# The gate and up projections of a two-FFN encoder layer, taken together in blocks of 512+512 columns, with three of eight pairs of row blocks multiplied by seven block products in place of eight

## The chip, the core and the metric

The kernel runs on one core of one Trainium2 chip. The metric is the time of one execution on the device in microseconds (us). The engines in play are TensorE (PE, matrix products into PSUM), VectorE (DVE), ScalarE (ACT), GpSimd (POOL, here above all the issuer of small transfers) and SyncE (SP, the issuer of the weight loads). The kernel before takes 1782.21 us (median of three runs, 1781.82 to 1783.28).

## What is computed

One encoder layer on 256 tokens of width 2048: a half-weighted SwiGLU feed-forward block, a mixer of two attention groups, a second half-weighted SwiGLU block, and a final norm. The change lies in the two feed-forward blocks, which the reference writes as

```python
def _swiglu(h, w_gu, w_down):
    g, u = jnp.split(h @ w_gu, 2, axis=-1)
    return (jax.nn.silu(g) * u) @ w_down
...
x = x + 0.5 * _swiglu(_rms_norm(x, ffn1_norm[l]), ffn1_w_gu[l], ffn1_w_down[l])
...
x = x + 0.5 * _swiglu(_rms_norm(x, ffn2_norm[l]), ffn2_w_gu[l], ffn2_w_down[l])
```

`w_gu` is 2048 x 11264: its left 5632 columns are the gate, its right 5632 the up projection. `w_down` is 5632 x 2048. All data are float32.

## The kernel before

**Precision.** Every float32 operand is split into a high part rounded to fp32r (`whi`, `xT_hi`, `hT_hi`; ACT casts) and a low part (`wlo`, `xT_lo`, `hT_lo`; DVE subtracts), both by `split` (L128 to L130). A product of two operands is three matmuls into one PSUM bank: high by high (L195), high by low (L196), low by high (L197). One matmul takes a 128x128 block of activations as the stationary operand and streams 512 weight columns.

**A block product.** `mm_block` (L158) runs over the rows of a weight matrix in pairs of 128-row blocks. Each pair of row blocks is one load by SP into a `raw` tile of 128x2x1024 (three such tiles), is split into two `whi` and two `wlo` tiles (four of each, so two pairs of row blocks can be split at a time), and is multiplied with both halves of the tokens (t = 0, 1) and both 512-column halves (b = 0, 1): 2 x 2 x 2 x 3 = 24 matmuls. After the last pair the four PSUM banks are read out by an `evac` function. PSUM has six banks for this (`ps_mm`) and two for everything else (`ps_x`).

**A feed-forward block.** `ffn` (L237) cuts the 5632 columns into groups of 1024 (the last has 512). For each group `gate` runs `mm_block` over the eight pairs of row blocks and ACT writes silu of the bank, scaled by the row norm, to `sg` (L246); `up` does the same with the up columns and DVE multiplies (L261) to `h`. Then `h` is turned: DVE transposes 32x32 squares to `near` (L274), POOL issues 16 small transfers to `turned` (L280), and `split` writes `hT_hi` and `hT_lo`. These steps stand in a list (`pending`) of which `pump` takes one per pair of row blocks. `down` multiplies `hT` with `w_down`, one group behind, in two halves of 1024 output columns, and DVE adds the banks to `x` (L232). The activations `xT_hi`, `xT_lo` have a pool of their own. In the first feed-forward block they are filled from transfers of `xT` through three `raw_x` tiles (`load_xT`, L324) while the first weights arrive.

**What sets the order.** The program is written in the order above, and a scheduler that follows its own timeline of the engines decides in which order each engine's queue gets the instructions (SP is kept in program order in the first gate, PE in the last half of the last `down`). On the chip every engine takes its queue in that fixed order and waits where an operand or a buffer is not ready.

## Time and profile before

| what | value |
|---|---|
| median of three runs | 1782.21 us |
| the profiled execution's own time | 1782.46 us |
| its span, first to last instruction | 1780.7 us |
| PE busy | 1767.7 us (99%) |
| DVE busy | 990.4 us (56%) |
| ACT busy | 829.2 us (47%) |
| granted TensorE clock | 0.999 of 2.4 GHz |
| transfers | 355.72 MB, 200 GB/s on average |

The span is what the trace shows; the 1.8 us by which the execution's own time exceeds it lie outside the first and the last instruction. "Busy" of PE includes matmuls that overlap in its pipeline, so the distance between matmuls, not the length of one, says how fast it runs.

### The profile page before, as it was taken

What the parts mean: (1) busy time and instruction counts of PE and PEld (TensorE: products, weight loads), DVE (VectorE), ACT (ScalarE), POOL (GpSimd) and SP (SyncE); (2) the same over time, 40 slices, a digit from 0 to 9 for tenths busy, and PEclk for the clock granted to TensorE, in tenths of its full rate; (3) what the DMA queues carried; (4) which work ended last, traced back from release to release, by engine and by line L of the source; (5) the groups of instructions that cost most, each with busy time, mean ns of one, the idle gap of its engine ahead of it and who ended that gap; (6) DMA issues with size and microseconds to landing.
All of it is one profiled execution on the core that took longest, in us unless ns stands there. A gap on an engine that the chain in (4) does not pass through costs nothing.

```text
span 1780.7 us, 20561 instructions
## 1 busy us (share of the span) xinstructions
PE 1767.7 (99%) x7864; PEld 1462.4 (82%) x7864; DVE 990.4 (56%) x1147; ACT 829.2 (47%) x1195; POOL 149.5 (8%) x267
## 2 busy tenths in 40 slices
PE   9999999999999999999999999999999999999998
PEld 7888888888888888888788888888888888888886
DVE  6454644645645556745566564555545546545556
ACT  6444443443443443746776454343443443344444
POOL 0010100100100101122110000101001001001010
PEclk9999999999999999999999999999999999999999
DMA  9565655655655676655455545666556556556573
GB/s 342 194 220 189 213 192 197 224 192 189 215 192 194 180 238 204 200 192 194 143 183 199 184 167 193 216 205 214 190 190 219 198 195 213 190 192 220 149 253 118
DMA packets 108418, 355.72 MB, mean 200 GB/s; under 512 B 10992, under 2 KB 15520, under 8 KB 108192
## 3 DMA queue, kind: packets, MB, share of 16 engines
q1 hardware_dynamic: 101360, 341.54, 57.7%
q0 software_dynamic: 6240, 11.57, 2.3%
q8 instruction: 61, 1.00, 0.2%
q10 hardware_dynamic: 720, 1.31, 0.2%
q14 instruction: 37, 0.30, 0.0%
HBM read 337.60 MB, written 2.10 MB: 191 GB/s over the span
## 4 chain that ended last, share of the span: by engine, by line
PE 95%; ACT 1%; DMA 1%; SPq 1%; DVE 1%; issue 1%; POOL 0%; POOLq 0%; ACTq 0%; DVEq 0%
PE psm L196 31%; PE psm L197 31%; PE psm L195 31%; DMA raw<-in_w_in 1%; SPq L456 1%; PE psx L142 0%; PE psx L549 0%; PE psx L564 0%; PE psx L584 0%; ACT heads L425 0%; ACT heads L443 0%; PE psx L513 0%; DMA gain_ffn_norm<-in_ffn_norm 0%; ACT q_sb L422 0%; ACT whi L129 0%
## 5 line engine op out<-in xcount | busy, mean ns | idle before, releaser
L130 DVE TENSOR_TENSOR wlo<-raw,whi 128x1024 fp32r<-128x1024 f32 (+1 forms) x676 | 757.6, 1153 | 703.1 <-ACT whi L129 699.4
L129 ACT CAST whi<-raw 128x1024 fp32r<-128x1024 f32 (+1 forms) x676 | 647.2, 996 | 843.8 <-PE psm L197 780.4
L196 PE MATMUL psm<-wlo,xT_hi 128*128 128x512 f32 x1696 | 659.1, 390 | 0.1
L197 PE MATMUL psm<-whi,xT_lo 128*128 128x512 f32 x1696 | 658.0, 390 | 0.0
L195 PE MATMUL psm<-whi,xT_hi 128*128 128x512 f32 x1696 | 587.7, 390 | 3.0 <-ACT whi L129 1.5
L195 PEld LDWEIGHTS psm<-whi,xT_hi 128*128 128x128 f32 x1696 | 318.2, 188 | 70.2 <-ACT xT_hi L330 2.4
L196 PEld LDWEIGHTS psm<-wlo,xT_hi 128*128 128x128 f32 x1696 | 318.4, 188 | 66.3 <-DVE wlo L130 0.5
L197 PEld LDWEIGHTS psm<-whi,xT_lo 128*128 128x128 f32 x1696 | 318.4, 188 | 65.8
L196 PE MATMUL psm<-wlo,hT_hi 128*128 128x512 f32 x836 | 323.9, 389 | 0.0
L197 PE MATMUL psm<-whi,hT_lo 128*128 128x512 f32 x836 | 323.6, 389 | 0.0
L195 PE MATMUL psm<-whi,hT_hi 128*128 128x512 f32 x836 | 295.4, 389 | 0.0
L280 POOL DMA_DIRECT2D turned<-near x192 | 101.3, 535 | 1204.6 <-DVE near L274 1020.0
L196 PEld LDWEIGHTS psm<-wlo,hT_hi 128*128 128x128 f32 x836 | 157.0, 188 | 32.2
L195 PEld LDWEIGHTS psm<-whi,hT_hi 128*128 128x128 f32 x836 | 157.0, 188 | 32.1
L197 PEld LDWEIGHTS psm<-whi,hT_lo 128*128 128x128 f32 x836 | 157.0, 188 | 31.9
L232 DVE SCALAR_TENSOR_TENSOR x<-psm,x 128x512 f32<-128x512 f32 (+1 forms) x113 | 74.5, 682 | 19.0 <-PE psm L197 17.6
L246 ACT ACTIVATE sg<-psm,rstd 128x512 f32<-128x512 f32 x44 | 28.6, 687 | 12.5 <-PE psm L197 12.5
L261 DVE SCALAR_TENSOR_TENSOR h<-psm,rstd,sg 128x512 f32<-128x512 f32 x44 | 31.6, 737 | 0.0
L130 DVE TENSOR_TENSOR hT_lo<-turned,hT_hi 128x512 fp32r<-128x512 f32 x44 | 30.1, 685 | 0.0
L104 POOL TENSOR_TENSOR rs<-ms,minus_half 128x4 f32<-128x4 f32 (+1 forms) x18 | 20.2, 1120 | 116.6 <-DVE ms L103 116.5
L120 ACT ACTIVATE junk<-x 128x512 bf16<-128x512 f32 (+1 forms) x33 | 20.3, 614 | 16.4 <-DVE x L232 14.2
L274 DVE STREAM_TRANSPOSE near<-h 128x1024 f32<-128x1024 f32 (+1 forms) x24 | 27.7, 1152 | 0.3
(102 smaller groups left out, 390.6 us busy)
## 6 DMA issues: line engine op xcount, KB each, us to landing
raw<-in_ffn_w_gu SPq DMA_DIRECT2D x158, 1024.0 KB, 5.0
raw<-in_ffn_w_down SPq DMA_DIRECT2D x88, 1024.0 KB, 5.1
raw<-in_w_in SPq DMA_DIRECT2D x32, 1024.0 KB, 5.2
raw<-in_ffn_w_gu SPq DMA_DIRECT2D x32, 512.0 KB, 3.7
raw<-in_w_out SPq DMA_DIRECT2D x16, 1024.0 KB, 5.0
turned<-near POOLq DMA_DIRECT2D x160, 64.0 KB, 4.5
raw<-in_w_in SPq DMA_DIRECT2D x8, 512.0 KB, 3.8
heads<-near SPq DMA_DIRECT2D x96, 32.0 KB, 1.9
```

The costliest lines, as they stand in the source:

```text
L104: nc.gpsimd.tensor_tensor(dst, ms[:, :width], minus_half[:, :width], op=ALU.pow)
L120: nc.scalar.activation(junk[:, :c1 - c0], x[t][:, c0:c1], AF.Square, scale=D ** -0.5, accum_out=p[:, n:n + 1])
L129: casts.append(nc.scalar.copy(hi, src))
L130: return nc.vector.tensor_tensor(lo, src, f32(hi), op=ALU.subtract)
L195: nc.tensor.matmul(o, xh, wh, start=k == 0, stop=False)
L196: nc.tensor.matmul(o, xh, wl, start=False, stop=False)
L197: nc.tensor.matmul(o, xl, wh, start=False, stop=k == nk - 1)
L232: nc.vector.scalar_tensor_tensor(x[t][:, s], ps[:, c0:c1], scale, x[t][:, s], op0=ALU.mult, op1=ALU.add)
L246: nc.scalar.activation(sg[t][:, b * 512:(b + 1) * 512], ps, AF.Silu, scale=norm.rstd[t][:, 0:1])
L261: nc.vector.scalar_tensor_tensor(h[t][:, s], ps, norm.rstd[t][:, 0:1], sg[t][:, s], op0=ALU.mult, op1=ALU.mult)
L274: nc.vector.transpose(near[:, t].rearrange("p q (k d) -> p q k d", d=B32), h[t][:, :width].rearrange("p (k q d) -> p q k d", q=Q, d=B32))
L280: nc.gpsimd.dma_start(turned[q * B32:(q + 1) * B32, :, i, :], near[i * B32:(i + 1) * B32, :, q, :])
```

## The change

The first 1024 columns of gate and up are computed as before, with the two halves of the rows in the pool `ht`. While its up part runs, the normalised activations are written once more in two new forms: for five of the eight pairs of row blocks `xs` (the first 128 tokens, the last 128, and their difference), for the other three `xp` (seven 128x128 combinations of the 2x2 square of row blocks and token halves). This is done by `spread`, `normalised`, `single_rows` and `paired_rows`.

The other 9 blocks of 512 columns of each feed-forward block go through `columns`: gate and up columns c0 to c0+511 together, eight loads of a `raw` tile, each now two transfers of one 128-row block with 512 gate and 512 up columns. A pair marked False in `PAIRS` is a single: it is split as before and multiplied in 4 x 2 x 3 = 24 matmuls into the banks `c12`, `c11`, `c3`, `c21`. A pair marked True is multiplied by Strassen's algorithm (Winograd's form): DVE forms four combinations of its four weight squares (`Ta`, `Tb`), these and three plain squares are split, and seven products of three matmuls are added to seven banks (21 matmuls); `p1`, `p6`, `p7` are the three further banks (`p7` lies in `ps_x`). When the last pair's products are done, `done` combines the seven banks with seven DVE adds, two DVE multiplies, one ACT copy and two silu to `h`. `h` is then turned by 512 columns, and takes the turned squares back itself.

```diff
+PAIRS = (False, False, True, False, False, True, False, True)
 MIX_SLOTS = 4
...
-    xt_p = ctx.enter_context(tc.tile_pool(name="xt", bufs=1))
...
+    def new_rows():
+
+        return (ht_p.tile([P, WB // P, T], F32R, name="hT_hi"), ht_p.tile([P, WB // P, T], F32R, name="hT_lo"))
+
+    def rows(sets):
+
+        def at(k, t):
+            return tuple(part[:, k % 8, t * P:(t + 1) * P] for part in sets[k // 8])
+        return at
+
...
+
+
+
+        with tc.tile_pool(name="ffn", bufs=1) as fp:
+            inner = ExitStack()
+            ip = inner.enter_context(tc.tile_pool(name="ffn_in", bufs=1))
+            w_pair = w_gu.rearrange("r (s f) -> r s f", s=2)
+            hT, turned_blocks = {}, set()
+            n_groups = (DFF + WB - 1) // WB
+
+
+            def turn_block(i, h):
+
+                near = fp.tile([P, NT, Q, P], F32, name="near")
+                turned = h.rearrange("p t (i f) -> p t i f", i=Q)
+
...
+                    to = 4 * (i % 2) + k
+                    hi, lo = (part[:, to:to + 2, :].rearrange("p k (i d) -> p i k d", d=B32)
+                              for part in hT[i // 2])
                     with tc.issue_after(splits[-1].ins):
                         split(hi, lo, src)
 
-                pending.extend(functools.partial(turn, t) for t in range(NT))
...
+            if before is None:
+                mm_block(rows(xT), NK, w_gu, 0, 0, WB, evac_gate)
+            else:
+                with tc.manual_schedule(engines={mybir.EngineType.SP}):
+                    mm_block(rows(xT), NK, w_gu, 0, 0, WB, evac_gate, lambda c: before(c, ip), after)
...
+            single = [k for c, pair in enumerate(PAIRS) if not pair for k in (2 * c, 2 * c + 1)]
+            paired = [c for c, pair in enumerate(PAIRS) if pair]
+            xs = [ip.tile([P, len(single), 3, P], F32R, name=f"xs{i}") for i in range(2)]
+            xp = [ip.tile([P, len(paired), 7, P], F32R, name=f"xp{i}") for i in range(2)]
+            rb = fp.tile([P, T], F32, name="rb")
+
+            def spread():
+                near = fp.tile([P, NT, Q, P], F32, name="near")
+                ps = ps_x.tile([P, 512], F32, name="psx")
+                for t in range(NT):
+                    nc.vector.tensor_scalar(near[:, t, 0, :], ident, 0.0, norm.rstd[t][:, 0:1],
+                                            op0=ALU.mult, op1=ALU.add)
+                    nc.tensor.transpose(ps[:, t * P:(t + 1) * P], near[:, t, 0, :], ident)
+                nc.scalar.copy(rb, ps[:, :T])
+
+            def normalised(c):
+                n = ip.tile([P, 2, 512], F32, name="Ta").rearrange("p j (a t) -> p (j a) t", t=T)[:, :2, :]
+                hi, lo = (f32(part[:, 2 * c % 8:2 * c % 8 + 2, :]) for part in xT[2 * c // 8])
+                nc.vector.tensor_tensor(n, hi, lo, op=ALU.add)
+                nc.vector.tensor_tensor(n, n, rb.unsqueeze(1).broadcast_to([P, 2, T]), op=ALU.mult)
+                return n
+
+            def single_rows(c):
+                n = normalised(c)
+                i = single.index(2 * c)
+                diff = ip.tile([P, 2, 512], F32, name="Tb")[:, 0, :2 * P].rearrange("p (k t) -> p k t", t=P)
+                nc.vector.tensor_tensor(diff, n[:, :, :P], n[:, :, P:], op=ALU.subtract)
+                hi, lo = (part[:, i:i + 2, 0:2, :].rearrange("p k a t -> p k (a t)") for part in xs)
+                split(hi, lo, n)
+                split(xs[0][:, i:i + 2, 2, :], xs[1][:, i:i + 2, 2, :], diff)
+
+            def paired_rows(c):
+                n = normalised(c)
+                i = paired.index(c)
+                z = ip.tile([P, 2, 512], F32, name="Tb")[:, 0, :].rearrange("p (a t) -> p a t", t=P)
+                a12, a22, a11, a21 = (n[:, j, t * P:(t + 1) * P] for j in range(2) for t in range(2))
+                nc.vector.tensor_tensor(z[:, 0, :], a21, a22, op=ALU.add)
...
+            pending.append(spread)
+            pending.extend(functools.partial(paired_rows if pair else single_rows, c)
+                           for c, pair in enumerate(PAIRS))
+            ready = []
+            pending.append(lambda: ready.append(True))
+            mm_block(rows(xT), NK, w_gu, 0, DFF, WB, evac_up, slots=2)
+            while not ready:
+                pump()
+            for b in range(2):
+                turn_block(b, h0[b])
+
+
+            def columns(i):
+                c0 = i * 512
+                order = ("c12", "c11", "c3", "c21", "p1", "p6")
+                bank = {n: ps_mm.tile([P, 512], F32, name="psm") for n in order}
+                bank["p7"] = ps_x.tile([P, 512], F32, name="psx")
+                t1 = fp.tile([P, WB], F32, name="sg0")
+                t2 = fp.tile([P, WB], F32, name="sg1")
+                c1, c22, u2, u3 = t1[:, :512], t1[:, 512:], t2[:, :512], t2[:, 512:]
+                h = fp.tile([P, NT, 512], F32, name="h", bufs=2)
+                begun = set()
+
...
+                def done(name):
+                    if name == "p1":
+                        nc.scalar.copy(c1, bank["p1"])
+                    elif name == "p6":
+                        add(u2, bank["p6"], c1)
+                    elif name == "p7":
+                        add(u3, bank["p7"], u2)
+                    elif name == "c12":
+                        add(u2, bank["c12"], u2)
+                        add(c22, bank["c12"], u3)
+                    elif name == "c11":
+                        add(c1, bank["c11"], c1)
+                        nc.scalar.activation(c1, c1, AF.Silu)
+                    elif name == "c3":
+                        add(u2, bank["c3"], u2)
+                        nc.vector.tensor_tensor(h[:, 0, :], u2, c1, op=ALU.mult)
+                    elif name == "c21":
+                        add(u3, bank["c21"], u3)
+                        nc.scalar.activation(u3, u3, AF.Silu)
+                        nc.vector.tensor_tensor(h[:, 1, :], u3, c22, op=ALU.mult)
+
+                for c, pair in enumerate(PAIRS):
+                    raw = raw_p.tile([P, 2, WB], F32, name="raw").rearrange("p j (s f) -> p j s f", s=2)
+                    w = []
+                    for j in range(2):
+                        k = 2 * c + j
+                        loads.append(nc.sync.dma_start(raw[:, j], w_pair[k * P:(k + 1) * P, :, c0:c0 + 512]))
+                    for j in range(2):
+                        hi = whi_p.tile([P, WB], F32R, name="whi").rearrange("p (s f) -> p s f", s=2)
+                        lo = wlo_p.tile([P, WB], F32R, name="wlo").rearrange("p (s f) -> p s f", s=2)
+                        n = 1 if pair and j == 1 else 2
+                        splits.append(split(hi[:, :n], lo[:, :n], raw[:, j, :n]))
+                        w.append([(hi[:, s], lo[:, s]) for s in range(2)])
+                    if not pair:
+                        def xk(j, a):
+                            i_ = single.index(2 * c + j)
+                            return xs[0][:, i_, a, :], xs[1][:, i_, a, :]
+                        for name, a_, s in (("c12", 1, 1), ("c11", 0, 0), ("c3", 2, 1), ("c21", 1, 0)):
+                            mm(name, [(xk(j, a_), w[j][s]) for j in range(2)], False)
+                        pump()
+                        continue
+                    i_ = paired.index(c)
+                    b21, b22, b11, b12 = (raw[:, j, s] for j in range(2) for s in range(2))
+                    tt = []
+                    ta = ip.tile([P, 2, 512], F32, name="Ta")
+                    tb = ip.tile([P, 2, 512], F32, name="Tb")
+
+                    flat = raw.rearrange("p j s f -> p (j s) f")
+                    nc.vector.tensor_tensor(ta, flat[:, 3:4, :].broadcast_to([P, 2, 512]), flat[:, 1:3, :],
+                                            op=ALU.subtract)
+                    nc.vector.tensor_tensor(tb[:, 0], b22, ta[:, 1], op=ALU.subtract)
+                    nc.vector.tensor_tensor(tb[:, 1], b21, tb[:, 0], op=ALU.subtract)
+                    for n, src in (("Ta", ta), ("Tb", tb)):
+                        hi = ip.tile([P, 2, 512], F32R, name=n + "_hi")
+                        lo = ip.tile([P, 2, 512], F32R, name=n + "_lo")
+                        splits.append(split(hi, lo, src))
+                        tt.extend((hi[:, s], lo[:, s]) for s in range(2))
+                    t3, t1_, t2_, t4 = tt
+                    xa = [(xp[0][:, i_, m, :], xp[1][:, i_, m, :]) for m in range(7)]
+                    a12, a22, a11, s1, s2, s3, s4 = xa
+                    product = {"p1": (a11, w[1][0]), "c11": (a12, w[0][0]), "c3": (s4, w[0][1]),
+                               "c21": (a22, t4), "c12": (s1, t1_), "p6": (s2, t2_), "p7": (s3, t3)}
+                    names = (("c11", "c3", "p1", "p7", "c12", "p6", "c21") if c < last else
+                             ("p1", "p6", "p7", "c12", "c11", "c3", "c21"))
+                    for m, name in enumerate(names):
+                        mm(name, [product[name]], c == last)
+                        if c == last:
+                            done(name)
+                        if m == 3:
+                            pump()
+                turn_block(i, h)
...
+                if final:
+                    inner.close()
+                    t_major = last_pools and last_pools(inner)
                 for half in range(2):
-                    evac = last_evac(half) if last and last_evac else add_to_x(half, 0.5)
...
+            for j in range(1, n_groups):
+                for i in range(2 * j, min(2 * j + 2, DFF // 512)):
+                    columns(i)
+                if j < n_groups - 1:
+                    down(j - 1)
+            down(n_groups - 2)
+            down(n_groups - 1)
...
+    xT = [new_rows(), new_rows()]
+
+    def load_xT(c, pool):
+
+        raw = pool.tile([P, 2, 512], F32, name=("Ta", "Tb")[c % 2]).rearrange("p j f -> p (j f)")[:, :2 * T]
+        raw = raw.rearrange("p (j t) -> p j t", j=2)
...
+            hi, lo = (part[:, k % 8, :] for part in xT[k // 8])
+            nc.scalar.activation(hi, raw[:, j, :], AF.Copy, scale=gain1[:, k:k + 1])
+            nc.vector.scalar_tensor_tensor(lo, raw[:, j, :], gain1[:, k:k + 1], f32(hi),
+                                           op0=ALU.mult, op1=ALU.subtract)
```

How the change moves the work is seen at one place on two engines. First the queue of DVE where a stretch of eight row-block pairs ends. Before, at the end of the first `up` (its `h` tiles are h0_497 and h1_498; wlo_788 and wlo_792 are the first split of the next gate):

```order
L130 TENSOR_TENSOR wlo_744<-raw_741,whi_743 128x1024
L130 TENSOR_TENSOR wlo_748<-raw_741,whi_747 128x1024
L130 TENSOR_TENSOR wlo_788<-raw_785,whi_787 128x1024
L130 TENSOR_TENSOR wlo_792<-raw_785,whi_791 128x1024
L261 SCALAR_TENSOR_TENSOR h0_497<-psm_509,rstd0_106,sg0_128 128x512
L261 SCALAR_TENSOR_TENSOR h1_498<-psm_516,rstd1_107,sg1_129 128x512
L261 SCALAR_TENSOR_TENSOR h0_497<-psm_523,rstd0_106,sg0_128 128x512
L274 STREAM_TRANSPOSE near_781<-h0_497 128x1024
L261 SCALAR_TENSOR_TENSOR h1_498<-psm_530,rstd1_107,sg1_129 128x512
L130 TENSOR_TENSOR wlo_827<-raw_824,whi_826 128x1024
```

The four reads of the banks and the first transpose stand together, between plain splits that are one pair of row blocks ahead.

Now the same queue at the change from one block of columns to the next in the first feed-forward block. In the block that ends, psm_1915 to psm_1918 are c12, c11, c3, c21, psm_1920 is p6 and psx_1921 is p7; raw_2262, raw_2299 and raw_2342 are the first three pairs of the next block, the third of them a Strassen pair:

```order
L130 TENSOR_TENSOR Tb_lo_2215<-Tb_2206,Tb_hi_2214 128x1024
L130 TENSOR_TENSOR wlo_2266<-raw_2262,whi_2265 128x1024
L434 TENSOR_TENSOR Ta_2353<-raw_2342 128x1024
L130 TENSOR_TENSOR wlo_2270<-raw_2262,whi_2269 128x1024
L384 TENSOR_TENSOR sg1_1923<-psm_1920,sg0_1922 128x512
L130 TENSOR_TENSOR wlo_2303<-raw_2299,whi_2302 128x1024
L436 TENSOR_TENSOR Tb_2354<-raw_2342,Ta_2353 128x512
L130 TENSOR_TENSOR Ta_lo_2359<-Ta_2353,Ta_hi_2358 128x1024
L384 TENSOR_TENSOR sg1_1923<-psx_1921,sg1_1923 128x512
L384 TENSOR_TENSOR sg0_1922<-psm_1916,sg0_1922 128x512
L130 TENSOR_TENSOR wlo_2307<-raw_2299,whi_2306 128x1024
L437 TENSOR_TENSOR Tb_2354<-raw_2342,Tb_2354 128x512
```

The combining adds (L384) are now woven into the splits of the next three pairs and into the weight combinations of the third. Next the queue of PE at the same two places. Before, the last matmuls of the first gate and the first of its `up` (psm_509, psm_516):

```order
L197 MATMUL psm_169<-whi_464,xT_lo_111 128x512
L196 MATMUL psm_176<-wlo_465,xT_hi_110 128x512
L197 MATMUL psm_176<-whi_464,xT_lo_111 128x512
L195 MATMUL psm_509<-whi_501,xT_hi_110 128x512
L196 MATMUL psm_509<-wlo_502,xT_hi_110 128x512
L197 MATMUL psm_509<-whi_501,xT_lo_111 128x512
L195 MATMUL psm_509<-whi_505,xT_hi_110 128x512
L195 MATMUL psm_516<-whi_501,xT_hi_110 128x512
L196 MATMUL psm_516<-wlo_502,xT_hi_110 128x512
```

The gate's last matmuls and the first of `up` follow each other with nothing between them, and `up` starts on two fresh banks.

Now the last products of the block that ends (psm_1918) and the first of the next (psm_2252 is its c12, psm_2253 its c11, psx_2258 its p7):

```order
L378 MATMUL psm_1918<-Tb_hi_2214,xp0_500 128x512
L380 MATMUL psm_1918<-Tb_lo_2215,xp0_500 128x512
L381 MATMUL psm_1918<-Tb_hi_2214,xp1_501 128x512
L378 MATMUL psm_2252<-whi_2265,xs0_498 128x512
L380 MATMUL psm_2252<-wlo_2266,xs0_498 128x512
L381 MATMUL psm_2252<-whi_2265,xs1_499 128x512
L378 MATMUL psm_2252<-whi_2269,xs0_498 128x512
L378 MATMUL psx_2258<-Ta_hi_2358,xp0_500 128x512
L380 MATMUL psm_2252<-wlo_2270,xs0_498 128x512
L381 MATMUL psm_2252<-whi_2269,xs1_499 128x512
L378 MATMUL psm_2252<-whi_2302,xs0_498 128x512
L378 MATMUL psm_2253<-whi_2265,xs0_498 128x512
```

PE no longer takes a pair of row blocks in one run: it starts the third pair's product (psx_2258) between the matmuls of the first, and begins the banks one after another, as they come free.

## Rows read from the trace of the kernel before

**Rows 1.** Part 1 and part 4 of the page: engines' busy time, chain that ended last

```profile
PE 1767.7 (99%) x7864; PEld 1462.4 (82%) x7864; DVE 990.4 (56%) x1147; ACT 829.2 (47%) x1195; POOL 149.5 (8%) x267
...
PE 95%; ACT 1%; DMA 1%; SPq 1%; DVE 1%; issue 1%; POOL 0%; POOLq 0%; ACTq 0%; DVEq 0%
```

**Rows 2.** The chain in order of time, first gate: start us, us, what

```profile
17.46 0.91 PE psm L195 x4
...
22.90 0.91 PE psm L195 x4
```

**Rows 3.** Instructions by line and shape: count, busy us, mean ns, idle before

```profile
L196 PE MATMUL psm<-wlo,xT_hi 128*128 128x512 f32 x1696 | 659.1, 390 | 0.1
...
L130 DVE TENSOR_TENSOR wlo<-raw,whi 128x1024 fp32r<-128x1024 f32 x588 | 697.6, 1222 | 655.4 <-ACT whi L129 654.6
...
L129 ACT CAST whi<-raw 128x1024 fp32r<-128x1024 f32 x588 | 593.0, 1052 | 783.0 <-PE psm L197 752.4 <-DMA raw<-in_w_in 8.9 <-issue 6.2
...
L130 DVE TENSOR_TENSOR wlo<-raw,whi 128x512 fp32r<-128x512 f32 x88 | 60.0, 691 | 47.7 <-ACT whi L129 44.8 <-PE psm L197 2.7
...
L232 DVE SCALAR_TENSOR_TENSOR x<-psm,x 128x512 f32<-128x512 f32 x111 | 73.7, 687 | 18.8 <-PE psm L197 17.4
...
L261 DVE SCALAR_TENSOR_TENSOR h<-psm,rstd,sg 128x512 f32<-128x512 f32 x44 | 31.6, 737 | 0.0
...
L130 DVE TENSOR_TENSOR hT_lo<-turned,hT_hi 128x512 fp32r<-128x512 f32 x44 | 30.1, 685 | 0.0
...
L274 DVE STREAM_TRANSPOSE near<-h 128x512 f32<-128x512 f32 x4 | 2.8, 702 | 0.0
...
L331 DVE SCALAR_TENSOR_TENSOR xT_lo<-raw_x,gain_ffn_norm,xT_hi 128x256 fp32r<-128x256 f32 x16 | 7.0, 480 | 0.1
...
L441 DVE TENSOR_TENSOR heads<-heads,swapped 128x128 f32<-128x128 f32 x8 | 2.3, 291 | 0.7
...
L142 PE MATMUL psx<-ident,x 128*128 128x128 f32 x64 | 9.2, 272 | 0.0
```

**Rows 4.** DVE in order of time, second gate: start, us, what, idle before

```profile
104.95 2.36 DVE L130 TENSOR_TENSOR wlo<-raw,whi 128x1024 fp32r<-128x1024 f32 x2 [3.08 <-ACT whi L129]
```

**Rows 5.** Stretch, us, busy of PE, PEld, DVE, ACT, POOL (count), clock, DMA share, GB/s

```profile
51.40:95.00 43.60, 43.60 (x194) 36.13 (x193) 21.73 (x21) 18.47 (x20) 0.00 (x0) 1.00 0.58 192
...
182.00:225.50 43.50, 43.50 (x194) 36.03 (x193) 27.33 (x30) 18.10 (x21) 8.43 (x16) 1.00 0.69 218
...
617.00:660.00 43.00, 43.00 (x191) 35.61 (x191) 24.17 (x35) 22.37 (x34) 0.00 (x0) 1.00 0.71 220
```

**Rows 6.** Part 6 of the page: DMA issues, KB each, us to landing

```profile
raw<-in_ffn_w_gu SPq DMA_DIRECT2D x158, 1024.0 KB, 5.0
...
raw<-in_ffn_w_gu SPq DMA_DIRECT2D x32, 512.0 KB, 3.7
...
turned<-near POOLq DMA_DIRECT2D x160, 64.0 KB, 4.5
```

**Rows 7.** Tile `near`: duration of an instruction, ns, min/median/max

```profile
L280 POOL DMA_DIRECT2D turned<-near x192: 533/533/612, 98.7 to 1723.7; - x192
```

**Rows 8.** In order of time, the start of the first gate

```profile
5.78 0.43 SPq L327 DMA_DIRECT2D raw_x<-in_xT  x1
...
6.23 0.89 DVE L331 SCALAR_TENSOR_TENSOR xT_lo<-raw_x,gain_ffn_norm,xT_hi 128x256 fp32r<-128x256 f32 x2
...
13.79 2.00 ACT L129 CAST whi<-raw 128x1024 fp32r<-128x1024 f32 x2 [1.73 <-DMA raw<-in_ffn_w_gu]
```

**Rows 9.** Busy by stretch, the start: columns as in Rows 5

```profile
6.20:12.00 5.80, 5.75 (x25) 4.75 (x26) 5.75 (x11) 5.74 (x12) 0.00 (x0) 1.00 1.05 391
...
12.00:51.00 39.00, 39.00 (x174) 32.31 (x173) 23.34 (x32) 26.31 (x44) 1.29 (x2) 1.00 0.90 335
```

171 lines of the change are left out of this document (75 added, 96 removed).

## The prediction

> **What bounds the kernel now.** Part 1 of the page comes first: TensorE is busy for 1767.7 of 1780.7 us, VectorE for 56%; part 4 agrees, with 95% of the chain of work that ended last on PE [rows 1]. A busy PE need not be a fast one, so the next view is the chain in order of time, in the first gate: one pair of row blocks starts at 17.46 us and the next at 22.90, 5.44 us for 24 matmuls, 0.2267 us each [rows 2]. The mean of 390 ns in the groups by line [rows 3] is longer because neighbours overlap; it prices nothing here. So the time is a number of matmuls times 0.2267 us, as long as the operands are ready.
>
> Whether they stay ready is read from the other engines. In a gate, DVE works 2.36 us on two splits and then waits 3.08 us for ACT's cast [rows 4], which in turn waits for PE to free the split tiles (752 of ACT's 783 us of idle time before this cast) [rows 3]. By stretches, an `up` of 43.6 us has 21.7 us of DVE work and a `down` of 43.5 us has 27.3 [rows 5]. DVE has room of about half its time, and this room is what the change spends.
>
> **What the change removes.** Each of the 9 blocks of columns per feed-forward block, 18 in all, has three Strassen pairs with 21 matmuls where 24 stood: 183 for 192. That is 18 x 9 = 162 matmuls, at 0.2267 us 36.7 us. A block's PE work falls from 43.5 to 41.5 us. On PE come four transposes in `spread`, at 0.272 us [rows 3] 1.1 us.
>
> **What it adds on DVE.** Prices are 1.18 us for a 128x1024 operation (half of 2.36 [rows 4]; 1.222 when it stands alone [rows 3]), 0.69 for 128x512, 0.687 from PSUM, 0.70 for a transpose, 0.685 for an `hT_lo` part [rows 3]. The sum over a block:
> - five singles, two splits each: 5 x 2.36 = 11.8;
> - three Strassen pairs: one and a half splits 1.87, `Ta` 1.18, `Tb` 2 x 0.69, two splits of combinations 2.36, so 6.79 each, 20.4;
> - `done`: seven adds and two multiplies, 9 x 0.69 = 6.2;
> - turning: 2 x 0.70 + 2 x 0.685 = 2.8.
>
> Together 41.2 us, and 42.1 if every operation has its full duration, against 41.5 of PE. In a block of columns DVE is thus as full as PE. Over two blocks and the `down` behind them it is not: that `down` leaves it 16 us (43.5 less 27.3) [rows 5], but with four `whi` and `wlo` tiles it can work only about two pairs of row blocks ahead, so little of this can be saved up. ACT has 24 us per block (ten casts at 1.05, three pairs at 3.8, the rest 3) and is not the bound [rows 3].
>
> **Where the adds wait.** The place to look at is the change of blocks, in the order of the queues. Seven banks are in use and the next block begins while they are read. Its first bank is the one that the ACT copy of p1 frees, its second is that of p6, and I take its third to be that of c11, from the wait that stands at its first matmul. From the end of the split `Tb_lo_2215` to the add on `psm_1916` that frees c11, DVE has five operations of 1.22 and four of 0.69: 8.9 us. PE has 36 matmuls from the one that needs `Tb_lo_2215` to the first in the third bank, 8.2 us. So PE stalls there about 0.7 us, or nothing where DVE was ahead; later in the block DVE is ahead again by the same count. Queued behind that wait on PE is everything else of the block; on DVE, the waits for ACT casts of `Ta` and `Tb` hold up the splits of the next pairs. I take 0.5 us per block, 9 us in all. The ends are 0, and 3.8: DVE's 42.1 us with the three casts of `Ta` at 1.05 us [rows 3] fully exposed makes a block of 45.3 us.
>
> **The first `up` of each feed-forward block** also makes `xs` and `xp`. DVE: 16 splits 18.9; five times `single_rows` at 2 x 0.69 + 0.48 + 0.69 + 0.48 = 3.03 (a 128x256 operation is 0.48), 15.2; three times `paired_rows` at 2 x 0.69 + 4 x 0.29 + 0.58 + 0.69 = 3.81, 11.4 (0.29 for 128x128; 0.58 is set between 0.48 and 0.69) [rows 3]; four reads at 0.737, 2.9. Sum 48.4 against 43.5 of PE, 4.9 too much. The two pairs of lead cover part; I take 3 us for each of the two, between 0 and 10 (10 if the next block's first Strassen preparation of 6.8 falls in front of the end too).
>
> **Loads.** A tile is now filled by two transfers of 512 KB with runs of 512 columns. The last group has such loads already: 3.7 us to landing against 5.0 for 1024 KB [rows 6], and a DMA share of 0.71 at 220 GB/s against 0.58 at 192 in an `up` [rows 5], 7% more engine time per byte. A block needs 8 MB in 41.5 us, 202 GB/s, so a share of about 0.65. I cost it at nothing: three `raw` tiles hide it. If that cover goes, it is a rival below.
>
> **The start.** `load_xT` has two tiles where it had three. The third `raw_x` transfer went out at 5.78 us; now it must wait on SP until the first tile has been read, and DVE does that from 6.23 to 7.12 [rows 8]. The weight loads stand behind it in SP's queue and slip by some 1.4 us. Loads are dense there (share 1.05, then 0.90), yet PE does not idle from 12 to 51 us [rows 9], and the third pair's cast starts at 13.79 [rows 8] for matmuls at 17.46 [rows 2]. I take 1 us, between 0 and 3.
>
> **The sum.** 1780.7 - 36.7 + 9 + 6 + 1.1 + 1 = 1761.1 us of span. The profiled execution's own time was 1.8 us over its span, and the median of the runs lies 0.25 us under it: 1762.6 us.
>
> **A rule against the change.** POOL issues each of the 192 transfers into `turned` in 533 ns, median and minimum alike, at most 612 [rows 7], although DVE operations of 1.2 us run beside them [rows 3]; DVE does not hold them up. By this row the 16 issues of a block take 8.6 us and land 4.5 later [rows 6], 13 us, while some 23 us of DVE work (15 x 1.22 + 7 x 0.69 by its queue) stand between the second transpose and the `hT_lo` part that needs them: hidden. If instead each issue waited out one DVE operation, 16 x (0.533 + 1.22) + 4.5 = 32.5 us, 9.5 too late per block, 171 in all, and 1933 us. The Trainium skill ("SBUF — State Buffer", section "SBUF: two separate sides") says that DVE and GpSimd share one port pair under an exclusive lock, held for a whole instruction, also by DVE operations with two SBUF inputs against a GpSimd operation that reads SBUF. By that rule the 1933 us would come about; the row speaks against it for these issues.
>
> **The rivals.**
> 1. Everything is hidden: DVE's lead of two pairs covers all block changes and the first `up`. 1780.7 - 36.7 + 1.1 = 1745.1 of span, 1746.6 us. For it: DVE's sum of 41.2 is under 41.5, and the order was woven to that end. Against: no reserve at all for a wait.
> 2. Slower: VectorE becomes the bound in the 18 blocks. Place: the Strassen pairs, where `Ta`, its cast and its split follow one another on two engines and block the splits behind them. Price: 45.3 us a block, 3.8 over PE, 68 in all, and 6 us in each first `up`: 1780.7 - 36.7 + 68.4 + 12 + 2.1 = 1826.5, so 1828 us. It decides from 1.6 us of stall per block on, where (36.7 - 8.1) / 18 is used up. For it: full durations alone make 42.1. Against: in the queue the cast and the split are parted by other work.
> 3. The loads: behind a Strassen pair DVE has two singles, 4.7 us, before it needs the tile that this pair frees; the load takes 5.0 [rows 6], 7% more 5.35. Two such places per block, 0.65 each, 23 us beside the stalls above: 1786 us, about no change. Against: DVE is ahead of PE there by some 4 us.
> 4. The port lock above, 1933 us.
>
> **Chances.** The forecast with its neighbours (own range 1750 to 1775 us) 0.56; everything hidden 0.13; VectorE as the bound 0.20, spread from no change up to 1830; the loads 0.09; the lock 0.02. Faster by over 0.2% (the least that a measurement of this kernel tells from no change): 0.56 + 0.13 + 0.01 = 0.70; within 0.2%: 0.07; slower: 0.23. The range of 8 in 10 goes from 1745, where all is hidden, to 1790, which takes in the loads and the milder part of rival 2, the ends of the unknown stalls being 0 and 3.8 us a block.
>
> **What the new profile would show.** PE's count falls from 7864 by 158, and a block of columns lasts 41.5 to 42.5 us, not 43.5 (rival 2: 44 to 46; rival 3: 43). DVE's busy time rises from 990 by some 380 us to about 77%. PE's waits name DVE (`wlo`, `Ta_lo`, or the bank adds) for about 15 us in total; over 35 would make rival 2 right, and waits on loads before `Ta` rival 3. `turned` issues stay at 533 ns. The forecast is wrong if a block of columns is over 43 us, or if PE is held for more than 10 us in a first `up`.

## The result, and the profile after

The changed kernel takes 1763.2 us (median of four runs, 1760.4 to 1770.4), 19 us less than before; the ratio of the runs is 0.9899, with a 95% interval of 0.9869 to 0.9928. The forecast was 1762.6. The profiled execution took 1760.4 us, the fastest of the four, with a span of 1758.6, 22.1 under the span of before.

First the page of after: engines' busy time, the chain that ended last, then groups by line (count | busy us, mean ns of one | idle us before, and what ended most of it), then DMA issues (KB, us to landing).

```profile
PE 1738.5 (99%) x7706; PEld 1430.3 (81%) x7706; DVE 1324.1 (75%) x1633; ACT 931.6 (53%) x1323; POOL 234.7 (13%) x427
...
PE 84%; DMA 6%; DVE 4%; ACT 2%; issue 2%; SPq 1%; DVEq 0%; POOL 0%; POOLq 0%; ACTq 0%
...
L271 POOL DMA_DIRECT2D h<-near x352 | 185.6, 535 | 1093.3 <-ACT whi L129 446.6
...
L434 DVE TENSOR_TENSOR Ta<-raw 128x1024 f32<-128x1024 f32 x54 | 66.2, 1225 | 64.0 <-DMA raw<-in_ffn_w_gu 63.9
...
L129 ACT CAST Ta_hi<-Ta 128x1024 fp32r<-128x1024 f32 x54 | 56.8, 1052 | 62.3 <-DVE Ta L434 61.6
...
L384 DVE TENSOR_TENSOR sg<-psm,sg 128x512 f32<-128x512 f32 x108 | 69.2, 681 | 0.0
...
raw<-in_ffn_w_gu SPq DMA_DIRECT2D x288, 512.0 KB, 4.8
```

Against [rows 1], PE has 158 matmuls less (7864 - 7706: 162 fewer products, four more transposes), DVE 334 us more work, and 6% of the chain is now transfers, where it was almost all PE. `Ta` costs the 1.22 us of [rows 3], but DVE sits idle 64 us in front of it, for the load of the weights: the wait that was to make rival 3 right. The bank adds (L384) wait for nothing. POOL's issues kept their price: 535 ns on average before and after, with the median of 533 of [rows 7]. A load of 512 KB lands in 4.8 us where the last group's took 3.7 [rows 6].

Next the busy time by stretches, each from the first matmul of a block of columns to the first matmul behind it, as in [rows 5]. The first two are the first couple of blocks, the third is the second block of the next couple, the fourth the second block of the last couple of this stage:

```profile
93.59:135.07 41.48, 41.48 (x184) 34.36 (x183) 35.83 (x41) 23.10 (x26) 11.56 (x22) 1.00 0.66 216
135.07:177.91 42.84, 41.82 (x185) 34.27 (x183) 40.20 (x46) 24.88 (x28) 12.78 (x26) 1.00 0.67 217
262.91:306.27 43.36, 42.44 (x184) 34.06 (x183) 38.61 (x45) 23.10 (x27) 8.45 (x16) 1.00 0.64 206
519.41:560.89 41.48, 41.48 (x184) 34.35 (x183) 37.42 (x44) 22.40 (x28) 8.42 (x16) 1.00 0.67 216
```

183 matmuls at 0.2267 us are 41.48 us: the first and the fourth block lose nothing, the second and the third 1.4 and 1.9 us. All first blocks of a couple in this stage take 41.48; what is lost is lost in blocks that follow a block, and up to 0.25 us in the `down` behind them.

By the last matmul of each stage, before and after, the 22.1 us are made up so:

| stage | matmuls removed, us | gained, us | lost, us |
|---|---|---|---|
| start and first gate | 0 | -0.1 | 0.1 |
| rest of the first feed-forward block | 18.4 | 13.0 | 5.3 |
| mixer | 0 | -1.9 | 1.9 |
| second feed-forward block | 18.4 | 14.2 | 4.1 |
| from the last matmul to the end (9.1 us, now 12.3) | 0 | -3.2 | 3.2 |
| sum | 36.7 | 22.0 | 14.7 |

What a stall of the third block looks like: the queue of DVE in order of time, then one row each of SP, ACT and PE (start us, duration us; in brackets the idle time before and what ended it).

```profile
253.23 1.82 DVE L130 TENSOR_TENSOR wlo<-raw,whi 128x1024 fp32r<-128x1024 f32 x2
...
258.75 1.23 DVE L130 TENSOR_TENSOR wlo<-raw,whi 128x1024 fp32r<-128x1024 f32 x1 [1.44 <-ACT whi L129]
262.16 1.23 DVE L434 TENSOR_TENSOR Ta<-raw 128x1024 f32<-128x1024 f32 x1 [2.18 <-DMA raw<-in_ffn_w_gu]
263.30 1.22 DVE L130 TENSOR_TENSOR wlo<-raw,whi 128x1024 fp32r<-128x1024 f32 x1
...
255.07 1.19 SPq L412 DMA_DIRECT2D raw<-in_ffn_w_gu  x2
...
263.49 1.05 ACT L129 CAST Ta_hi<-Ta 128x1024 fp32r<-128x1024 f32 x1 [2.39 <-DVE Ta L434]
...
264.59 0.50 PE L378 MATMUL psx<-Ta_hi,xp 128*128 128x512 f32 x1 [0.62 <-ACT Ta_hi L129]
```

This is the change of blocks that the document shows in the queues of DVE and PE: `Ta_2353<-raw_2342` stands behind one split of the new block, and PE's psx_2258 behind four matmuls. raw_2342 takes the tile of raw_2194, the last Strassen pair of the block before. DVE reads that tile for the last time in the split that ends at 253.23 + 1.82 = 255.05, SP issues the load at 255.07, and `Ta` starts at 262.16: 7.1 us for two transfers of 512 KB. DVE stands 2.2 us with the next splits queued behind, and PE begins its matmul at 264.59, 1.0 us after the one before instead of 0.23. The two other second blocks of this stage that lose show the same: `Ta` waits 1.45 and 2.00 us for its load (at 135.41 and 390.57 us), and PE's matmul comes 1.4 and 0.8 us after the one before.

The end: the last drain on POOL, before and after (instruction: count: ns min/median/max, first and last start us).

```profile
L718 POOLq DRAIN  x3: 46/102/6722, 1773.2 to 1780.4; - x3
```

```profile
L885 POOLq DRAIN  x3: 46/102/9908, 1747.9 to 1758.4; - x3
```

The long one is the first of the three. Before, it ended at 1779.9 together with the last store (SP was through at 1779.5). Now SP is through at 1754.3 and POOL's drain at 1757.8: 3.5 us in which the kernel waits for it alone.

### The profile page after: what moved, and what is told of

Read it like the earlier page. It is cut to its first block, busy times and chain, and to the rows that moved or that the text cites. A ratio compares the mean times of both kernels' runs of the same rounds, so it can differ in the third digit from the quotient of the medians.

```text
span 1758.6 us, 21325 instructions
## 1 busy us (share of the span) xinstructions
PE 1738.5 (99%) x7706; PEld 1430.3 (81%) x7706; DVE 1324.1 (75%) x1633; ACT 931.6 (53%) x1323; POOL 234.7 (13%) x427
## 4 chain that ended last, share of the span: by engine, by line
PE 84%; DMA 6%; DVE 4%; ACT 2%; issue 2%; SPq 1%; DVEq 0%; POOL 0%; POOLq 0%; ACTq 0%
PE psm L203 16%; PE psm L204 16%; PE psm L202 16%; PE psm L380 11%; PE psm L381 11%; PE psm L378 11%; DMA raw<-in_ffn_w_gu 5%; DVE wlo L130 2%; SPq L618 1%; DVE Ta L434 1%; ACT whi L129 1%; PE psx L378 1%; DMA raw<-in_w_in 1%; PE psx L380 1%; PE psx L381 1%
## 5 line engine op out<-in xcount | busy, mean ns | idle before, releaser
L203 PE MATMUL psm<-wlo,hT_hi 128*128 128x512 f32 x1252 | 484.7, 391 | 0.1
L204 PE MATMUL psm<-whi,hT_lo 128*128 128x512 f32 x1252 | 482.9, 390 | 0.0
L202 PE MATMUL psm<-whi,hT_hi 128*128 128x512 f32 x1252 | 433.0, 390 | 3.2 <-ACT whi L129 1.8
L271 POOL DMA_DIRECT2D h<-near x352 | 185.6, 535 | 1093.3 <-ACT whi L129 446.6
L380 PE MATMUL psm<-wlo,xs 128*128 128x512 f32 x720 | 279.8, 389 | 0.0
L381 PE MATMUL psm<-whi,xs 128*128 128x512 f32 x720 | 279.6, 389 | 0.0
L203 PEld LDWEIGHTS psm<-wlo,hT_hi 128*128 128x128 f32 x1252 | 235.1, 188 | 50.7 <-DVE wlo L130 2.5
L204 PEld LDWEIGHTS psm<-whi,hT_lo 128*128 128x128 f32 x1252 | 235.1, 188 | 47.8
L378 PE MATMUL psm<-whi,xs 128*128 128x512 f32 x720 | 253.2, 390 | 0.4 <-ACT sg L388 0.3
L378 PEld LDWEIGHTS psm<-whi,xs 128*128 128x128 f32 x720 | 135.1, 188 | 30.4 <-DVE sg L384 1.6
L380 PEld LDWEIGHTS psm<-wlo,xs 128*128 128x128 f32 x720 | 135.1, 188 | 28.2
L381 PEld LDWEIGHTS psm<-whi,xs 128*128 128x128 f32 x720 | 135.2, 188 | 28.1
L434 DVE TENSOR_TENSOR Ta<-raw 128x1024 f32<-128x1024 f32 x54 | 66.2, 1225 | 64.0 <-DMA raw<-in_ffn_w_gu 63.9
L384 DVE TENSOR_TENSOR sg<-psm,sg 128x512 f32<-128x512 f32 x108 | 69.2, 681 | 0.0
```

What stands on the lines that cost most here:

```text
L202: nc.tensor.matmul(o, xh, wh, start=k == 0, stop=False)
L203: nc.tensor.matmul(o, xh, wl, start=False, stop=False)
L204: nc.tensor.matmul(o, xl, wh, start=False, stop=k == nk - 1)
L271: nc.gpsimd.dma_start(turned[q * B32:(q + 1) * B32, :, i_, :], near[i_ * B32:(i_ + 1) * B32, :, q, :])
L378: nc.tensor.matmul(bank[name], xh, wh, start=name not in begun, stop=False)
L380: nc.tensor.matmul(bank[name], xh, wl, start=False, stop=False)
```

## Experiments on the loads

Theory: the Strassen pairs hold their raw tile until DVE has made `Ta`, `Tb` and the splits, so the third next load starts too late. Rival: DVE's work is the bound and its waits for loads only fill idle time. There was not room for a fourth raw tile, so `near` was laid into the tile `sg1` that the combinations use (in `spread`, into `Tb`); a control did only that. The control:

```diff
-                near = fp.tile([P, NT, Q, P], F32, name="near")
+                near = fp.tile([P, WB], F32, name="sg1").rearrange(...)
```

> Control for the fourth raw tile: only `near` moved into the place of other tiles, three raw tiles. Both theories: as the changed kernel, 1760 to 1766 us, waits for raw before Ta of 55 to 75 us; if sharing the place costs something by itself, it shows here as 1 to 3 us.

And with the fourth tile:

```diff
+                    own = len(loads) // 2 % 4 == 3
-                    raw = raw_p.tile([P, 2, WB], F32, name="raw")...
+                    raw = ip.tile([P, 2, WB], F32, name="raw4") if own else raw_p.tile([P, 2, WB], F32, name="raw")
```

> The changed kernel with a fourth raw tile for the column blocks (every fourth load has a tile of its own; `near` shares another tile's place to make room). Loads theory (a pair of 7 products holds its raw tile until Ta and Tb are made, so the next load starts late and the next Ta waits for it): VectorE's waits for raw before Ta fall from 63.9 us to under 15, the time that the 18 column blocks take beyond their matmuls falls from about 9 us to under 3, and the time comes to 1754 to 1758 us. Rival (VectorE's own work is the bound in these blocks, the wait for raw only fills its idle time): the waits for raw may fall, but the blocks lose 8 to 10 us as before, time 1761 to 1765 us.

Measured: the control 1785.4 us (ratio to before 1.0016, 1.0005 to 1.0028), the fourth tile 1771.7 (0.9937, 0.9924 to 0.9950). Both miss their expectations, because the shared tile costs far more than the 1 to 3 us allowed for it. The group of the bank adds, which waited for nothing in the changed kernel, in the control:

```profile
L384 DVE TENSOR_TENSOR sg<-psm,sg 128x512 f32<-128x512 f32 x108 | 69.2, 682 | 16.0 <-DMA h<-sg 15.9
```

The adds stand behind the transfers that read `near`. In the kernel with the fourth tile this happens above all at the first `down` of a stage, where the turns of the first two blocks are both outstanding: 29.9 us for matmuls that take 21.8. Some 1.8 us of this follow the wait in the list below: from within it on, the granted clock is at 0.5 (1.2 GHz) for 6.8 us, and the first eight matmuls behind it come 0.43 us apart. Its waits from 170 to 215 us, on DVE and PE (us in total, times, longest):

```profile
DVE sg L384 <- DMA h<-sg: 6.9, 1, 6.9
...
PE psm L202 <- DVE sg L384: 6.1, 1, 6.1
```

Beside that the blocks ran as the loads theory has it: the second blocks of the first stage took 41.55, 41.67 and 41.54 us. Against the control the fourth tile is worth 13.7 us, but by the distances between matmuls only some 4 us of this lie in the column blocks, where the loads theory has them. About 9.7 us lie at the two first `down`s, which lose 10.5 and 13.0 us in the control and 8.1 and 5.7 with the fourth tile; why the shared tile costs less there with a fourth raw tile was not tested.

A first attempt to take the new stall away took `near` and `sg1` later in the program:

```diff
+                    if c == last:
+                        t1 = fp.tile([P, WB], F32, name="sg0")
+                        t2 = fp.tile([P, WB], F32, name="sg1")
```

> The fourth raw tile again, with the tile that `near` shares with the combinations (sg1) taken later in the program: `near` when its transpose is written, sg1 at the last pair of a column block. What was lost at the first `down` of a stage with the shared tile (8.1 us: 29.88 us for 96 matmuls that take 21.76) should be gone, since the first blocks' combinations no longer stand behind the moves of h0. Loads theory: the second column block of each couple takes 41.5 to 41.7 us as with the fourth tile before (41.55, 41.67, 41.54 there, 42.83, 43.37, 42.67 with three), nothing is lost at the `down` behind it, 4 to 5 us less per feed-forward stage than the changed kernel, time 1753 to 1757 us. Rival (the late wait was only moved and the blocks lose it elsewhere): 1760 to 1765 us.

It failed: 1772.6 us (0.9937, 0.9923 to 0.9950), the first `down` still at 29.9 us, with the same wait:

```profile
DVE sg L382 <- DMA h<-sg: 7.3, 1, 7.3
```

The second put the first two turns in two different tiles and their transfers into the first block of columns:

```diff
+            first, second = turn_block(0, h0[0], "sg0"), turn_block(1, h0[1], "sg1")
+            pending.extend(first[:3] + second[:2] + first[4:6] + second[2:4] + first[6:] + second[4:])
```

> The fourth raw tile for the third time, the stall that came with it taken away otherwise: the tiles that the turns of the first two blocks share are two (sg0 and sg1), and both turns are written within the first column block, so that its combinations find both free. Loads theory: no column block loses more than 0.3 us and the first `down` takes 21.8 us instead of 29.9; against the fourth tile before, 8 us per feed-forward stage less: 1753 to 1758 us. Rival (what is lost at the first `down` has another cause than the shared tile): the first `down` keeps its 29 to 30 us, 1770 to 1773 us.

It took 1756.7 us (1755.6 to 1757.0; 0.9854, 0.9836 to 0.9871), the first `down` 21.8. The stretches are the second and the fourth block of columns, the same as the second and the third row of the changed kernel above:

```profile
135.19:177.30 42.11, 41.83 (x184) 34.24 (x183) 37.23 (x43) 23.32 (x29) 8.45 (x16) 1.00 0.68 217
262.30:303.90 41.60, 41.60 (x184) 34.27 (x183) 36.81 (x42) 22.96 (x27) 8.46 (x16) 1.00 0.67 218
```

42.1 and 41.6 for 42.8 and 43.4, and nothing lost at the `down` behind them; the first second-block missed the 0.3 us by another 0.3. At the change of blocks looked at above, in this kernel:

```profile
255.99 1.23 DVE L435 TENSOR_TENSOR Ta<-raw 128x1024 f32<-128x1024 f32 x1 [0.99 <-DMA raw<-in_ffn_w_gu]
```

`Ta` starts 6.2 us earlier (5.6 us, counted from the block's first matmul) and still waits 1 us for its load, but with that lead nobody waits for it. The scheduler made new queues here, so the lead is not the only difference: PE takes the product of `Ta` as the 15th matmul of this block, and took it as the fifth before. At the change in the first couple it is the eighth in both kernels; there it started 1.2 us late in the changed kernel and starts on time in this one. A control with this order and three raw tiles was not run. So a wait that a profile names costs only where the chain behind it reaches PE: DVE's waits before `Ta` fell just from 63.9 to 53.5 us, not under 15 as was expected of the fourth tile, while PE's long gaps (what matmuls that start over 0.28 us apart take beyond 0.227) in the first stage fell from 4.7 us to 0.9. In the second feed-forward block, however, they stayed (3.8 us, now 5.0), and what PE waits for there, from 1060 to 1750 us, is another thing:

```profile
PE psm L379 <- DVE wlo L130: 1.6, 2, 0.9
PE psm L377 <- ACT sg L387: 1.0, 1, 1.0
```

There the scheduler wove the queues in another order, and the splits are late, not the loads. The loads theory fits the first stage; what is left in the second are late splits, which is nearer to its rival. By spans this kernel is 3.5 us faster than the changed one; the 6.5 us between the medians are more because the profiled execution of the changed kernel was its fastest.

## Experiments on the end

Theory: POOL's last drain grows with the number of transfers it issued (192 before, 352 now). The kernel before, with each transfer in two:

```diff
-                        nc.gpsimd.dma_start(turned[q * B32:(q + 1) * B32, :, i, :],
-                                            near[i * B32:(i + 1) * B32, :, q, :])
+                        for t in range(NT):
+                            nc.gpsimd.dma_start(turned[q * B32:(q + 1) * B32, t, i, :],
+                                                near[i * B32:(i + 1) * B32, t, q, :])
```

> The kernel before with each turn transfer split in two (384 transfers issued by POOL instead of 192). Tail theory: from the last POOL operation to the end 6.2 us become about 10, the end after the last matmul grows from 8.8 by 3 to 4 us, time 1785 to 1787 us. Rival (the longer end of the changed kernel has another cause): the end stays at 8.8 us, time 1782 us within 0.1%.

And the changed kernel with the transfers on SP:

```diff
-                        nc.gpsimd.dma_start(turned[q * B32:(q + 1) * B32, :, i_, :],
+                        nc.sync.dma_start(turned[q * B32:(q + 1) * B32, :, i_, :],
```

> The changed kernel with the 288 turn transfers of the feed-forward stages issued by SP instead of POOL. Tail theory (POOL's last semaphore comes later the more transfers POOL has issued: 0.46 us behind SP with 192, 3.63 us with 352): POOL signals within 0.6 us of SP, the end after the last matmul falls from 12.0 to about 9 us, 3 us less. What stands against a gain: the transfers wait for `near` in SP's queue in front of weight loads; if that blocks loads, the waits for raw before Ta grow over 100 us and the time is 1765 to 1780 us; if not, 1759 to 1761 us. Rival for the tail (it is another part of the end, such as the pools that are opened last): the end stays at 12.0 us.

The drains, first of the kernel before with 384 transfers, then of the changed one with none of them on POOL:

```profile
L719 POOLq DRAIN  x3: 46/102/2631, 1774.5 to 1781.3; - x3
```

```profile
L885 POOLq DRAIN  x3: 51/93/911, 1804.0 to 1810.8; - x3
```

The theory fell: with 384 transfers the drain took 2.6 us, less than with 192, and the time stayed (1783.4 us, 0.9999, 0.9990 to 1.0008). Without transfers it took 0.9 us and the end 8.6, so it is POOL's transfers, but not their sum. Moving them to SP (all 352; my expectation says 288) cost far more than it gave, and more than the 1780 us that I had allowed: 1813.0 us (1.0171, 1.0157 to 1.0184). In the queues of that kernel:

```profile
SPq L271 <- DVE near L265: 77.5, 14, 8.7
...
ACT hT_hi L129 <- DMA h<-near: 90.3, 19, 8.4
...
PE psm L378 <- ACT whi L129: 24.6, 11, 3.8
```

SP waits for the transpose with weight loads behind it. I had expected this to show as longer waits before `Ta`; those fell to 18 us. ACT waits instead, for the transfers and for loads, and its casts hold PE.

Four numbers of transfers, 0, 192, 352 and 384, fit one pattern: the drain follows the remainder by 128 (0, 64, 96, 0). That was tested by issuing 32 more in the middle of the first feed-forward block. The same kernel places the attention's result tiles at the start of their pool, for the mixer's 1.9 us: there the 384 matmuls that read these tiles were spaced wider than all others.

```diff
+        oTs = [tuple(mp.tile([P, WB // P, T], F32R, name=f"oT_{n}{i}") for n in ("hi", "lo")) for i in range(2)]
...
+                        whole = last_evac is not None or i not in (8, 9)
+                        for t in (slice(0, NT),) if whole else (slice(0, 1), slice(1, NT)):
```

> The changed kernel with two edits at two places far apart, each read from its own stretch. (1) POOL issues 32 transfers more (the turns of blocks 8 and 9 of the first feed-forward stage in two halves each), 384 instead of 352. The last drain of POOL took 6.72 us with 192 transfers, 9.91 with 352, 2.63 with 384 and 0.91 with none, which is a line if what counts is the remainder by 128 (64, 96, 0, 0). Remainder theory: the drain falls to 1 to 3 us and the end after the last matmul from 12.3 to 8.8 us, 3.5 us less by issuing more. Rival (the drain grows with what POOL issued): 10 to 11 us, the end at 12.3 us or later. (2) The tiles of the attention's result (oT) stand at the start of their pool instead of behind the tables. Place theory: the matmuls that read them, spaced 231 to 235 ns, come back to 227 ns, 2 us less in the mixer; rival (not the place): they stay at 231 to 235 ns.

1756.5 us (0.9855, 0.9837 to 0.9872). The drain, and matmuls of the same stretch in the changed kernel and in this one:

```profile
L887 POOLq DRAIN  x3: 46/102/2638, 1747.9 to 1754.7; - x3
```

```profile
1021.13 0.39 PE L203 MATMUL psm<-wlo,oT_hi 128*128 128x512 f32 x1
...
1023.46 0.40 PE L204 MATMUL psm<-whi,oT_lo 128*128 128x512 f32 x1
```

```profile
1021.13 0.39 PE L202 MATMUL psm<-whi,oT_hi 128*128 128x512 f32 x1
...
1023.40 0.39 PE L203 MATMUL psm<-wlo,oT_hi 128*128 128x512 f32 x1
```

Both held. Issuing more shortened the drain from 9.9 to 2.6 us and the end to 8.6, so the drain does not grow with the number of transfers. That it follows the remainder by 128, and not another rule that puts these four numbers in the same order, is not shown: the test used 384 again, a number already seen. Ten matmuls take 2.33 us in the changed kernel, 2.27 here: 233 ns, back to 227; the mixer's stretch is shorter by 2.1 us, 1.8 of them in the 106 us of these matmuls. Other things move the mixer too: with four pairs and this edit (below) it takes 327.7 us, as long as in the changed kernel. Why the place counts, and what POOL does in the drain, no run shows.

## Experiments on the number of Strassen pairs

> One Strassen pair of row blocks (the last one) instead of three: 54 matmuls less than before instead of 162, 12.24 us. All theories: no wait for raw in the blocks (no two Strassen pairs follow each other), so the time is before - 12.2 plus the fixed costs (POOL's end 3.2 us, mixer 2 us, start 0.3 us): 1774 to 1777 us. If the rewriting by blocks costs more by itself (columns of 512 + 512, loads of 512 KB): above 1778 us.

> Two Strassen pairs (the fourth and the last) instead of three: 108 matmuls less than before, 24.5 us. Loads theory (two Strassen pairs near each other hold two of three raw tiles): with three ordinary pairs between them the loads have time, the second blocks lose under 0.5 us, time 1762 to 1765 us, level with three pairs. Rival (each Strassen pair costs a stall of its own): the loss is two thirds of that with three pairs, time 1767 to 1770 us.

> Four Strassen pairs (every second pair) instead of three: 216 matmuls less than before, 49 us. VectorE theory: a fourth pair adds to VectorE in a block 1.22 (Ta) + 1.38 (Tb) + 2.44 (their low parts) less 0.54 (half a low part), 4.5 us, on 39 us, with 40.8 us of matmuls: VectorE has work for over 43 us, PE waits 2 to 5 us in most blocks and the fourth pair gives nothing back, 1765 to 1800 us. Rival (the lighter `down` stages, 24 us of VectorE work in 43.5, even it out): 1752 to 1758 us.

```diff
-PAIRS = (False, False, True, False, False, True, False, True)
+PAIRS = (False, False, False, False, False, False, False, True)   # one
+PAIRS = (False, False, False, True, False, False, False, True)    # two
+PAIRS = (False, True, False, True, False, True, False, True)      # four
```

| pairs | time, us | ratio to before (interval) | second block of the first two couples, us | matmuls alone |
|---|---|---|---|---|
| 1 | 1776.3 | 0.9962 (0.9948 to 0.9975) | 42.8, 42.8 | 42.84 |
| 2 | 1767.3 | 0.9910 (0.9897 to 0.9924) | 42.2, 42.2 | 42.16 |
| 3 | 1763.2 | 0.9899 (0.9869 to 0.9928) | 42.8, 43.4 | 41.48 |
| 4 | 1764.0 | 0.9890 (0.9877 to 0.9904) | 45.2, 42.5 | 40.80 |

With four pairs the last four matmuls of the first couple come behind the first of the `down`; the 45.2 us are the 44.3 to that first one and these four. Each pair takes 12.24 us from PE. With one and two pairs the blocks of the table lose under 0.1 us, and of all blocks one in the second stage with two pairs loses more (1.1 us). The intervals of two, three and four pairs overlap, so what a pair is worth is read from the traces: both feed-forward blocks together lose 0.8, 2.1, 9.5 and 22.1 us with one to four pairs, so the third pair brings some 5 us of its 12 (4 by the medians) and the fourth nothing. With one pair the time is as expected (1774 to 1777). With two pairs the expectation for the blocks held but for that one block, and the time did not (1767 for 1762 to 1765): it lies in the rival's range, though the rival's stalls are not there; its profiled execution, of 1766.3 us, begins 1.7 us late in the way that the last section shows. With four the time fell 1 us short of the range for the VectorE theory and far from its rival's.

## The edits together

> The three edits that moved something, together: the fourth raw tile (third form), 384 transfers issued by POOL, oT at the start of its pool; three Strassen pairs. If they add up: 1756.7 (the fourth tile alone) - 3.65 (POOL's last drain) - 2 (384 matmuls spaced 227 instead of 233 to 235 ns) = 1751 us, between 1749 and 1753, a ratio to before of 0.9826. If they share a cause (the same waits counted twice): 1754 to 1757 us.

> The same with four Strassen pairs (every second pair): 12.24 us less of matmuls, 4.5 us more VectorE work in a block. VectorE theory (with the loads out of the way VectorE, 43.5 us of work beside 40.8 us of matmuls, is the bound of a block, and the `down` stages even out only a part): the second column blocks lose 1 to 4 us, the time is level with three pairs, 1747 to 1755 us. Rival (what four pairs lost was the loads alone): 18 x 0.68 = 12 us less than three pairs, 1738 to 1741 us.

Three pairs: 1751.9 us (1751.0 to 1753.2), ratio 0.9826, 0.9812 to 0.9839, as the sum had it; this version beats both kernels. Four pairs: 1753.9 us (0.9834, 0.9820 to 0.9847). So with the loads improved the fourth pair still gives nothing. The time lies in the range of the VectorE theory, but the blocks do not lose as either theory had it. Two stretches of the kernel with four pairs, the second block of the first couple and of the next:

```profile
134.92:178.81 43.89, 42.83 (x185) 34.34 (x185) 42.38 (x50) 25.95 (x30) 8.46 (x16) 1.00 0.63 204
...
267.63:308.43 40.80, 40.80 (x181) 33.78 (x180) 37.34 (x43) 22.61 (x27) 8.45 (x16) 1.00 0.66 218
```

The later block takes 40.80 us, its 180 matmuls and nothing else, with DVE busy for 37.3. In the first couple DVE is busy for 42.4 of 43.9. From the first couple to the `down` behind it PE's long gaps make 8 us in the first stage and 9 in the second; behind that they make 0.6 and 0.2. The fourth pair's 12 us thus come in and are lost again in the first couple of each stage, where the turns of two blocks and the first splits meet behind an `up` in which DVE was busy 41.1 of 43.5 us. In the first stage 4.4 of the 8 us lie at the first `down`, and there it is again the shared tile: DVE's adds wait 3.0 us for its transfers, and behind that wait the granted clock is at 0.5 for 3.4 us. The row of this `down`, whose 96 matmuls take 21.76 us elsewhere:

```profile
178.81:205.07 26.26, 23.67 (x97) 19.11 (x96) 17.76 (x23) 9.96 (x12) 1.14 (x3) 0.94 0.52 179
```

So VectorE is full in the first couples, but not all of what is lost there is its work; four pairs with a lighter first couple, or without the shared tile, were not tried.

## Why the prediction was right, and where it was not

- **The matmuls removed, 36.7 us:** right. PE's count fell by 158, and blocks that wait for nothing take 41.48 us, 183 times 0.2267.
- **The block changes, 0.5 us each, 9 us:** the size was right, the place and the cause were not. 5.3 us in the first stage and 4.1 in the second are 0.5 us per block, but in the first stage as 1.2 to 1.9 us in three blocks and next to none in the other six. By my own sign (wrong if a block is over 43 us) one block of 18 was over, with 43.4. I placed the stall at the third bank, behind DVE's adds; those wait for nothing, and PE's weight loads wait for them 1.6 us in all, in four blocks. In the first stage it is above all the load of the third pair, the mechanism of rival 3, which I had priced at 23 us beside the stalls and given 0.09. Its tile is freed as I said, by a Strassen pair; what I mis-sized is the lead of DVE, which covers all first blocks and the last couples.
- **Loads at nothing:** wrong for the same reason. I read 3.7 us for a 512 KB load from the last group; in pairs they land in 4.8, 7.1 from the first issue to the use.
- **The first `up`, 6 us:** 43.5 us and nothing lost in the first feed-forward block, 43.8 and 0.3 in the second. Of the 48.4 us of work that I set against this `up`, DVE did 39.0 in it and some 3 in the gate before; the rest went behind it or was counted too high.
- **The start, 1 us:** 0.1. Whatever the delay in SP's queue is, PE does not see it.
- **Not in the sum at all:** 3.2 us at the end and 1.9 in the mixer. I took both stretches as unchanged since no line of the diff does work there; the first depends on how many transfers POOL has issued, the second, as far as the runs show, on where a pool puts tiles that had to move.
- **The total:** 14.7 us lost in the profiled execution, 17.1 forecast. The first `up`, the start and most of the transposes (6 + 1 + 1.1 us) were too much, and 5.1 us were not seen at all; that the median agrees within 0.6 us is partly luck. The runs themselves lie between 1760.4 and 1770.4 us, and by spans the forecast was 1761.1 and the profiled execution 1758.6.
- **Against rival 2:** in the first stage no block took more than 43.4 us, where it had 45.3; DVE was busy 334 us more (380 forecast), and that suffices with three pairs. **Against rival 4:** POOL's issues stayed at 535 ns with DVE at 75%, so the port rule that I quoted from the Trainium skill ("SBUF — State Buffer", section "SBUF: two separate sides") does not show on these issues.
- **The test by waits:** I wrote that PE's waits would name DVE for 15 us. In the two feed-forward blocks PE's matmuls name ACT's `Ta_hi` for 3.0 us and little else, of 8.5 us in gaps of over 0.28 us from matmul to matmul. More stands in the rows of the weight loads (PEld): `Ta_hi` 5.0 us, DVE's `Tb_lo` 1.8, the bank adds 1.6 and, in these blocks, `wlo` 1.6. So DVE is named for about 5 us, not 15.

```profile
PEld psx L378 <- ACT Ta_hi L129: 5.0, 5, 1.4
...
L378 PEld LDWEIGHTS psm<-whi,xs 128*128 128x128 f32 x720 | 135.1, 188 | 30.4 <-DVE sg L384 1.6
```

## What to carry to other kernels

When work is moved from a full engine to a half-full one, look at what the second engine's longer queue holds: here not its own time but the tiles it frees late, and so the loads. Try the trade in steps: with two pairs the blocks gave nearly the full price, the third pair brought some 5 of its 12 us, the fourth nothing. And read the start and the end of the trace as stages of their own, for what is issued earlier can be paid there.
